# Sparse attention on Trainium2: the value products of a head pair in one burst behind its last probability copy

## The chip, the cores and the metric

The kernel runs on one core of a Trainium2 chip. The metric is the device time of one execution in microseconds. The kernel before takes 2106.75 us, the median of three runs (2106.66 to 2107.36).

## What is computed

The reference is a decoder trunk of two layers on 512 tokens of width 1024, batch 1. Each layer has a hybrid mixer with three branches (sparse attention, HGRN2, gated delta net), a cross attention over 256 memory tokens and a gated MLP with a causal convolution. The change touches only the sparse attention, the branch `nsa_attention`, of which this is the core:

```python
s_cmp = jnp.einsum('bsghd,bngd->bghsn', q, kc).astype(F32) * scale
p_cmp = masked_softmax(s_cmp, cmp_mask)
o_cmp = jnp.einsum('bghsn,bngd->bsghd', p_cmp.astype(vc.dtype), vc)
...
    p = masked_softmax(s, mask)
    return jnp.einsum('bgqhn,bgqnd->bgqhd', p.astype(vg.dtype), vg)
...
p_win = masked_softmax(s_win, wmask[None, :, None, None])
o_win = jnp.einsum('bnghqk,bnkgd->bnqghd', p_win.astype(vw.dtype), vw).reshape(B, S, G, HG, DH)
...
o = g[..., 0:1] * o_cmp + g[..., 1:2] * o_sel + g[..., 2:3] * o_win
```

There are 8 heads of width 64 in 2 groups. Each head's output is a gated sum of three attentions: over 31 compressed blocks, over the selected blocks and over a window. With 512 tokens the selection takes every block and the window every earlier token, so both of these are causal attentions over at most 512 keys.

## The kernel before

**Stages.** Work is tiled into 128 partitions and blocks of 128 tokens. In each layer the mixer runs the gated delta net and HGRN2, then the sparse attention (`nsa_attn`, called from `mixer`), then the gates and branch products that merge the three branches. Dense projections are matmuls of 512 columns (`pd` tiles, helpers `dense` and `mm3`). Each weight block of 128x512 is loaded by SyncE's queue into `wr`, cast by ScalarE to `wh` (line 242) and its remainder is formed by VectorE in `wl` (line 245). Twelve matmuls use one such block. All matmuls go through the helper `mm`, so they stand under line 235. Below, a "dense step" is one matmul into `pd`.

**Order.** The kernel is written as a dataflow. A scheduler with priorities sets the order on each engine when the program is built. Dense matmuls that are due after the attention fill TensorE wherever the attention's own next matmul isn't yet ready by that scheduler's estimate. On each engine the order is then fixed, and an engine waits at the head of its queue.

**The attention.** `nsa_attn` loops over four blocks of queries (i = 0 to 3) and in each over four head pairs (j; one head of each group, g = 0 and 1). That makes 16 rounds in a layer, 32 in all; below, "round" is one (i, j). At the start of a block, compressed scores of all heads are made (`kcT`, eight matmuls), normalized, transposed (line 1065) and copied to `pc`. A round then does this:

- For each g and each of the two attentions br (0 selected, 1 window), scores of width (i+1)*128 (at least 256) are made in a PSUM tile `pa`: two matmuls and a mask product of the bf16 constants `identb` and `negb`. VectorE takes the negated maximum (line 1083) and scales it, ScalarE takes the exponential with its sum into a tile `pr` from the pool `chain`.
- VectorE scales each `pr` by the gate over the sum. TensorE transposes it in i+1 pieces (line 1099) into a PSUM tile `pt`. ScalarE copies that to a further `chain` tile, `pT`.
- The output `po` is a PSUM tile `pa`. Its first two products are those of the compressed values (`vcpad`, one for each g), then come the value products against `tok`: for br 0 and 1, for each key block k, for g 0 and 1. Group 0 writes partitions 0 to 63, group 1 partitions 64 to 127, so each of these matmuls has 64 output rows. ScalarE copies `po` to `y[j]`.

PSUM has three buffers of `pd`, two of `pa` and three of `pt`; `chain` has 36. The products with `vcpad` and `tok` and the transposes are fp32. Each of those products stands as two records in the trace, and each transpose as one.

```python
def mm(out_, lhsT, rhs, start=True, stop=True):
    TE.matmul(out_, lhsT, rhs, start=start, stop=stop, skip_group_check=True)
def pa():
    return pp.tile([P, T], F32, tag="pa", name=f"pa_{uid[0]}", bufs=2)
def pt():
    return pp.tile([P, T], F32, tag="pt", name=f"pt_{uid[0]}", bufs=3)
```

Of the kernel before, what the change touches and what calls it, by code (L numbers as in the profile page):

```python
# [13 lines left out]
AF = mybir.ActivationFunctionType  # L14
# [5 lines left out]
P = 128  # L20
# [178 lines left out]
def tile_trunk(ctx, tc, a, out, dbg=None):  # L199
    nc = tc.nc  # L200
    dbg = dbg or {}
    V, S, G, TE = nc.vector, nc.scalar, nc.gpsimd, nc.tensor
# [7 lines left out]
    def tl(tag, bufs, shape=(P, T), dt=F32):  # L210
        uid[0] += 1
        return sb.tile(list(shape), dt, tag=tag, name=f"{tag}_{uid[0]}", bufs=bufs)

    def chain():
        return tl("chain", NCHAIN)
# [5 lines left out]
    def pa():  # L221
        uid[0] += 1
        return pp.tile([P, T], F32, tag="pa", name=f"pa_{uid[0]}", bufs=2)

    def pt():
        uid[0] += 1
        return pp.tile([P, T], F32, tag="pt", name=f"pt_{uid[0]}", bufs=3)

    def small(n, dt=F32):
        if n <= 16:  # L230
            return tl("tiny", 40, (P, 16), dt)[:, :n]
        return tl("small", 10, (P, 64), dt)[:, :n]

    def mm(out_, lhsT, rhs, start=True, stop=True):
        TE.matmul(out_, lhsT, rhs, start=start, stop=stop, skip_group_check=True)  # L235
# [5 lines left out]
    def act(o, i, f=AF.Copy, **kw):  # L241
        S.activation(o, i, f, **kw)  # L242

    def tt(o, x, y, op, eng=None):
        (eng or V).tensor_tensor(o, x, y, op)  # L245

    def ts(o, x, s1, s2, op0, op1=None, eng=None):
        if op1 is None:
            (eng or V).tensor_scalar(o, x, s1, None, op0)
        else:  # L250
            (eng or V).tensor_scalar(o, x, s1, s2, op0, op1)
# [6 lines left out]
    def mark(name):  # L258
        if "mark" in dbg:
            dbg["mark"](name, nc)  # L260
# [193 lines left out]
    vcpad = [cst.tile([P, 4, 64], F32, name=f"vcpad{i}") for i in range(2)]  # L454
# [571 lines left out]
    def nsa_attn(l, tok, y, st):  # L1026
        KH, KL, QS, kcT, r8 = (st[k] for k in ("KH", "KL", "QS", "kcT", "r8"))
        mark("attn")
        gall = tl("gall", 1, (P, NT, 24))
        act(gall, tok[:, :, TOK_G:TOK_G + 24], AF.Tanh, scale=0.5)  # L1030
        ts(gall, gall, 0.5, 0.5, MUL, ADD)

        for i in range(NT):
            qs_ = slice(i * P, (i + 1) * P)
            sc = pa()
            for j in range(4):
                for g_ in range(2):
                    mm(sc[:, (4 * g_ + j) * 64:(4 * g_ + j + 1) * 64], QS[j, g_][:, qs_],
                       kcT[:, g_].rearrange("p a n -> p (a n)"))
            e = tl("tg", NTG)[:, :256].rearrange("p (h n) -> p h n", h=8)  # L1040
            m3 = cmpm[:, i:i + 1, :].to_broadcast([P, 8, 32])
            pen = tl("cmpn", 1, (P, 32))
            ts(pen, cmpm[:, i, :], -NEG, NEG, MUL, ADD)
            p3 = pen[:, None, :].to_broadcast([P, 8, 32])
            s4 = sc.rearrange("p (h a n) -> p h a n", a=2, n=32)
            tt(e, s4[:, :, 0], p3, ADD)
            tt(e, e, s4[:, :, 1], ADD)
            b8 = lambda t_, n_=32: t_.rearrange("p (h o) -> p h o", o=1).to_broadcast([P, 8, n_])
            tt(e, e, b8(r8[:, i]), MUL)
            mx = small(8)  # L1050
            V.tensor_reduce(mx, e, AX.X, MAX)
            tt(e, e, b8(mx), SUB)
            act(e, e, AF.Exp)
            tt(e, e, m3, MUL)
            dn = small(8)
            V.tensor_reduce(dn, e, AX.X, ADD)
            ts(dn, dn, 1e-30, None, MAX)
            V.reciprocal(dn, dn)
            g3 = gall[:, i, :].rearrange("p (h b) -> p h b", b=3)
            cf = small(8)  # L1060
            tt(cf, dn, g3[:, :, 0], MUL)
            tt(e, e, b8(cf), MUL)
            ps = pt()
            for g_ in range(2):
                TE.transpose(ps[:, g_ * P:(g_ + 1) * P], e[:, g_ * 4:g_ * 4 + 4, :].rearrange("p h n -> p (h n)"), ident)
            pc = tl("tg", NTG)
            act(pc[:, :256], ps[:, :256])

            for j in range(4):
                hd = {}  # L1070
                W = (i + 1) * P
                WM = max(W, 256)
                den = small(4)
                prs = []
                for g_ in range(2):
                    for br in range(2):
                        q_ = QS[j, g_][:, qs_]
                        ps = pa()
                        mm(ps[:, :WM], q_, KH[br, g_][:, :WM], stop=False)
                        mm(ps[:, :WM], q_, KL[br, g_][:, :WM], start=False, stop=False)  # L1080
                        mm(ps[:, i * P:W], identb, negb, start=False, stop=True)
                        nm = small(1)
                        V.tensor_reduce(nm, ps[:, :W], AX.X, MAX, negate=True)  # L1083
                        rc = r8[:, i, 4 * g_ + j:4 * g_ + j + 1]
                        tt(nm, nm, rc, MUL)
                        pr = chain()
                        act(pr[:, :W], ps[:, :W], AF.Exp, bias=nm, scale=rc, accum_out=den[:, 2 * g_ + br:2 * g_ + br + 1])
                        prs.append(pr)
                V.reciprocal(den, den)
                g4 = gall[:, i, :].rearrange("p (g j b) -> p g j b", g=2, b=3)[:, :, j, 1:]  # L1090
                tt(den.rearrange("p (g b) -> p g b", g=2), den.rearrange("p (g b) -> p g b", g=2), g4, MUL)
                for g_ in range(2):
                    for br in range(2):
                        x_ = 2 * g_ + br
                        pr = prs[x_]
                        ts(pr[:, :W], pr[:, :W], den[:, x_:x_ + 1], None, MUL)
                        pst = pt()
                        for k in range(i + 1):
                            TE.transpose(pst[:, k * P:(k + 1) * P], pr[:, k * P:(k + 1) * P], ident)  # L1099
                        pT = chain()  # L1100
                        act(pT[:, :W], pst[:, :W])
                        hd[g_, br] = pT
                po = pa()
                o_ = [po[g_ * 64:(g_ + 1) * 64, :P] for g_ in range(2)]
                for g_ in range(2):
                    mm(o_[g_], vcpad[g_][:, j, :], pc[:, g_ * P:(g_ + 1) * P], start=True, stop=False)
                for br, off in ((0, TOK_VS), (1, TOK_VW)):
                    for k in range(i + 1):
                        for g_ in range(2):
                            mm(o_[g_], tok[:, k, off + g_ * 64:off + g_ * 64 + 64], hd[g_, br][:, k * P:(k + 1) * P],  # L1110
                               start=False, stop=(br == 1 and k == i))
                act(y[j][:, qs_], po[:, :P])
                yield

# [92 lines left out]
    def mixer(l, norm):  # L1207
# [68 lines left out]
        for _ in nsa_attn(l, tok, ya, st):  # L1276
            pass
# [165 lines left out]
```

## Time and profile before

| what | value |
|---|---|
| median of three runs | 2106.75 us |
| the profiled execution's own time | 2107.62 us |
| its span, first to last instruction | 2105.8 us |
| TensorE matmuls busy | 2055.6 us, 98% |
| TensorE weight loads busy | 1611.4 us, 77% |
| VectorE busy | 1436.6 us, 68% |
| ScalarE busy | 952.2 us, 45% |
| GpSimd busy | 132.7 us, 6% |
| mean granted TensorE clock | 0.995 of full speed |

The profiled execution stands 0.87 us over the median. Its own time is 1.8 us more than its span. The attention's rounds lie at about 369 to 556 us in the first layer and 1400 to 1590 us in the second. A matmul's end in the profile is modelled, so a record's length holds time in which the next one already runs. What a matmul costs is read from the step between starts.

### The profile page before, as it was taken

To read this page: it belongs to the slowest core of one execution; us is meant where nothing else is said; L and a number is where in the kernel's file an instruction comes from. 1 tells how busy PE (TensorE), PEld (TensorE's weight loads), DVE (VectorE), ACT (ScalarE), POOL (GpSimd) and SP (SyncE) were. 2 spreads that over 40 slices of the span, in tenths; PEclk is the share of its full clock that TensorE was granted. 3 is DMA by queue.
4 is the path that set the end of the run, shared out by engine and by line. 5 is a ranking of instruction groups with operands and counts; after the bars stand their busy time and mean duration, and the time that the engine had idled before them with its cause. 6 is when DMAs were issued, how large, how long until landed. Compare 5 with 4: busy or idle time off the path is not lost. (4 is left out here: it accounts for less than half of the span.)

```text
span 2105.8 us, 31108 instructions
## 1 busy us (share of the span) xinstructions
PE 2055.6 (98%) x11396; PEld 1611.4 (77%) x11400; DVE 1436.6 (68%) x3052; ACT 952.2 (45%) x1868; POOL 132.7 (6%) x120
## 2 busy tenths in 40 slices
PE   8999999999999999999999998999999999999999
PEld 7877777777786788888888776777778767888887
DVE  6774898666656887377548469975666578755873
ACT  6434434555545544244444244445554454433442
POOL 2000122000010100000000003110000110000000
PEclk9999999999999999999999999999999999999999
DMA  7332222111241233323432312121113412333333
GB/s 238 90 101 71 76 72 61 56 51 46 61 136 47 94 94 95 95 95 96 119 107 78 101 41 91 56 76 51 41 46 91 128 58 90 96 93 98 95 98 108
DMA packets 118826, 180.91 MB, mean 86 GB/s; under 512 B 19920, under 2 KB 40528, under 8 KB 118672
## 3 DMA queue, kind: packets, MB, share of 16 engines
q1 hardware_dynamic: 91008, 158.64, 24.8%
q10 hardware_dynamic: 27584, 19.97, 3.2%
q8 instruction: 90, 1.47, 0.3%
q14 instruction: 64, 0.52, 0.1%
q0 software_dynamic: 80, 0.29, 0.0%
HBM read 170.21 MB, written 8.65 MB: 85 GB/s over the span
## 5 line engine op out<-in xcount | busy, mean ns | idle before, releaser
L235 PE MATMUL pd<-act,wh 128*128 128x512 f32 x3008 | 984.4, 403 | 1.4 <-DVE act L254 1.0
L242 ACT ACTIVATE wh<-wr 128x512 fp32r<-128x512 f32 (+3 forms) x600 | 368.1, 614 | 660.2 <-PE pd L235 578.3
L235 PEld LDWEIGHTS pd<-act,wh 128*128 128x128 f32 x3008 | 559.9, 189 | 133.6 <-issue 15.6
L235 PE MATMUL pd<-act,wl 128*128 128x512 f32 x1504 | 605.8, 403 | 3.0 <-DVE wl L245 3.0
L245 DVE TENSOR_TENSOR wl<-wr,wh 128x512 fp32r<-128x512 f32 (+3 forms) x600 | 409.7, 684 | 209.5 <-ACT wh L242 202.3
L235 PE MATMUL pd<-chain,wh 128*128 128x512 f32 x1344 | 426.1, 397 | 3.4 <-DVE gate L254 3.2
L235 PEld LDWEIGHTS pd<-act,wl 128*128 128x128 f32 x1504 | 284.1, 189 | 72.4 <-issue 7.1
L235 PEld LDWEIGHTS pd<-chain,wh 128*128 128x128 f32 x1344 | 251.9, 189 | 63.0 <-DVE gate L254 3.6
L235 PE MATMUL pd<-chain,wl 128*128 128x512 f32 x672 | 267.3, 398 | 0.9 <-DVE wl L245 0.9
L245 DVE TENSOR_TENSOR gate<-pd,rb 128x512 f32<-128x512 f32 x168 | 116.1, 691 | 103.9 <-PE pd L235 101.7
L235 PE MATMUL pa<-chain,chain 128*64 128x64 f32 (+7 forms) x1248 | 158.0, 294 | 4.6 <-DVE tiny L1340 3.8
L235 PEld LDWEIGHTS pd<-chain,wl 128*128 128x128 f32 x672 | 126.9, 189 | 32.2 <-DVE wl L245 2.9
L254 DVE SCALAR_TENSOR_TENSOR gate<-gate,vec,gate 128x510 f32<-128x510 f32 (+1 forms) x176 | 131.7, 750 | 18.9 <-ACT gate L242 15.9
L235 PEld LDWEIGHTS pa<-chain,chain 128*64 128x64 f32 (+3 forms) x1248 | 109.7, 162 | 43.1 <-issue 16.1
L1083 DVE TENSOR_REDUCE tiny<-pa 128x1 f32<-128x128 f32 (+3 forms) x128 | 61.2, 488 | 81.5 <-PE pa L235 81.2
L242 ACT ACTIVATE chain<-pa,tiny,r 128x128 f32<-128x128 f32 (+3 forms) x128 | 78.8, 616 | 60.9 <-DVE tiny L245 56.4
L245 POOL TENSOR_TENSOR chain<-chain,t 128x512 f32<-128x512 f32 x30 | 40.9, 1362 | 1015.7 <-ACT t L242 1015.7
L242 ACT ACTIVATE chain<-pt 128x512 f32<-128x512 f32 (+3 forms) x156 | 61.0, 444 | 65.0 <-PE pt L1099 37.1
L242 ACT ACTIVATE gate<-gate,vec 128x512 f32<-128x512 f32 x88 | 63.9, 726 | 27.0 <-DVE gate L245 27.0
L245 DVE TENSOR_TENSOR chain<-pd,chain 128x512 f32<-128x512 f32 x64 | 43.7, 688 | 37.0 <-PE pd L235 36.6
L235 PE MATMUL pa<-chain,tok 128*64 128x128 f32 x704 | 62.3, 282 | 0.0
L254 DVE SCALAR_TENSOR_TENSOR t<-t,gate 128x512 f32<-128x512 f32 x88 | 60.6, 688 | 1.9 <-ACT t L242 0.4
(238 smaller groups left out, 2006.4 us busy)
## 6 DMA issues: line engine op xcount, KB each, us to landing
wr<-in_w_fm SPq DMA_DIRECT2D x184, 256.0 KB, 2.7
wr<-in_w_up SPq DMA_DIRECT2D x176, 256.0 KB, 2.6
wr<-in_w_dn SPq DMA_DIRECT2D x64, 256.0 KB, 2.7
wr<-in_w_mix SPq DMA_DIRECT2D x32, 256.0 KB, 2.7
wr<-in_w_dn SPq DMA_DIRECT2D x32, 192.0 KB, 2.4
wr<-in_w_tk SPq DMA_DIRECT2D x16, 272.0 KB, 3.0
wr<-in_w_kv SPq DMA_DIRECT2D x16, 256.0 KB, 3.5
chain<-in_cmp_w SPq DMA_DIRECT2D x16, 256.0 KB, 4.0
```

The lines of the kernel that those rows point to most:

```text
L235: TE.matmul(out_, lhsT, rhs, start=start, stop=stop, skip_group_check=True)
L242: S.activation(o, i, f, **kw)
L245: (eng or V).tensor_tensor(o, x, y, op)
L254: V.scalar_tensor_tensor(o, x, s, y, op0, op1)
L1083: V.tensor_reduce(nm, ps[:, :W], AX.X, MAX, negate=True)
```

## The change

In every round the value products become one block behind the last of the four probability copies, and the compressed products move from its front to its end. Concretely:

- The copy of the transposed probabilities goes back into `pr`, no longer into a new `chain` tile.
- `po` is a `pt` tile, one of the three buffers of the transposes, no longer a `pa` tile, one of the two buffers of the scores.
- The first product of each group (br 0, k 0) gets an added wait on the fourth copy (g 1, br 1), and carries the start flag.
- The `vcpad` products come last.

```diff
-                        pT = chain()
-                        act(pT[:, :W], pst[:, :W])
-                        hd[g_, br] = pT
-                po = pa()
+                        copied = S.activation(pr[:, :W], pst[:, :W], AF.Copy)
+                        hd[g_, br] = pr
+                po = pt()
                 o_ = [po[g_ * 64:(g_ + 1) * 64, :P] for g_ in range(2)]
-                for g_ in range(2):
-                    mm(o_[g_], vcpad[g_][:, j, :], pc[:, g_ * P:(g_ + 1) * P], start=True, stop=False)
                 for br, off in ((0, TOK_VS), (1, TOK_VW)):
                     for k in range(i + 1):
                         for g_ in range(2):
-                            mm(o_[g_], tok[:, k, off + g_ * 64:off + g_ * 64 + 64], hd[g_, br][:, k * P:(k + 1) * P],
-                               start=False, stop=(br == 1 and k == i))
+                            m_ = TE.matmul(o_[g_], tok[:, k, off + g_ * 64:off + g_ * 64 + 64],
+                                           hd[g_, br][:, k * P:(k + 1) * P],
+                                           start=(br == 0 and k == 0), stop=False, skip_group_check=True)
+                            if br == 0 and k == 0:
+                                tc.add_manual_dep(m_.ins, copied.ins.name, mybir.DependencyInfo(
+                                    mybir.DependencyClass.Sync, mybir.DependencyReason.DATA), reason="one burst")
+                for g_ in range(2):
+                    mm(o_[g_], vcpad[g_][:, j, :], pc[:, g_ * P:(g_ + 1) * P], start=False, stop=True)
                 act(y[j][:, qs_], po[:, :P])
```

The scheduler lays the whole attention out anew. Outside the attention, and the dense matmuls around it, the order on TensorE stays. The next rows show three places. They are of the round i = 2, j = 2 of the first layer.

TensorE before, around the compressed products (`vcpad`) of this round, into `pa_4740`:

```order
L235 MATMUL pd_5665<-chain_3168,wl_5662 128x512
L235 MATMUL pa_4740<-tg_4505,vcpad_86 64x128
L235 MATMUL pa_4740<-tg_4505,vcpad_87 64x128
L235 MATMUL pd_5675<-act_160,wh_5678 128x512
L235 MATMUL pd_5675<-act_161,wh_5678 128x512
```

They stand alone between dense matmuls, some 20 rows ahead of the round's other products. TensorE before, at the round's last transposes (line 1099) and its first value products (`tok`):

```order
L1099 MATMUL pt_4727<-cm,chain_4699 128x128 x3
L1099 MATMUL pt_4734<-cm,chain_4708 128x128 x3
L235 MATMUL pa_4740<-chain_4717,tok_533 64x128
L235 MATMUL pd_5675<-act_291,wh_5678 128x512
L235 MATMUL pa_4740<-chain_4731,tok_533 64x128
L235 MATMUL pa_4740<-chain_4717,tok_533 64x128
L235 MATMUL pa_4740<-chain_4731,tok_533 64x128
```

The first value product stands right behind the transposes, alone; a dense matmul parts it from the other eleven. TensorE with the change, at the same place of the same round:

```order
L1099 MATMUL pt_4685<-cm,chain_4659 128x128 x3
L1099 MATMUL pt_4691<-cm,chain_4668 128x128 x3
L235 MATMUL pd_5556<-act_246,wh_5559 128x512
L235 MATMUL pd_5556<-act_247,wh_5559 128x512
L235 MATMUL pd_5556<-act_246,wl_5560 128x512
L1107 MATMUL pt_4696<-chain_4641,tok_533 64x128
L1107 MATMUL pt_4696<-chain_4659,tok_533 64x128
```

Three dense matmuls now stand between the last transpose and the first value product. The end of the same block, with the change:

```order
L1107 MATMUL pt_4696<-chain_4650,tok_533 64x128
L1107 MATMUL pt_4696<-chain_4668,tok_533 64x128
L235 MATMUL pt_4696<-tg_4473,vcpad_86 64x128
L235 MATMUL pt_4696<-tg_4473,vcpad_87 64x128
L235 MATMUL pa_4740<-chain_2600,chain_3745 128x384
L235 MATMUL pa_4740<-chain_2601,chain_3745 128x384
```

The twelve value products and the two compressed ones are one block, and scores of the next round follow. ScalarE with the change, in the same round (`chain<-pt` at line 1100 is a probability copy, `chain,tiny<-pa` the exponential of a score):

```order
L242 ACTIVATE wh_5577<-wr_5575 128x512
L1100 ACTIVATE chain_4641<-pt_4673 128x384
L1100 ACTIVATE chain_4650<-pt_4679 128x384
L1100 ACTIVATE chain_4659<-pt_4685 128x384
L1100 ACTIVATE chain_4668<-pt_4691 128x384
L242 ACTIVATE chain_4729,tiny_4712<-pa_4722,tiny_4726,r_769_3697 128x384
```

The four copies follow each other, as they did before; what moved is that each writes the tile that was transposed.

## Rows read from the trace of the kernel before

**Rows 1.** View by stretch: PE, PEld, DVE, ACT (POOL) busy, clock, DMA share, GB/s.

```profile
369.00:556.00 187.00, 186.76 (x1173) 137.51 (x1173) 117.28 (x337) 103.50 (x269) 0.00 (x0) 1.00 0.15 47
556.00:640.00 84.00, 84.00 (x377) 67.97 (x376) 52.65 (x99) 37.02 (x60) 7.75 (x6) 1.00 0.40 128
...
1400.00:1590.00 190.00, 189.55 (x1184) 139.20 (x1183) 119.63 (x342) 103.34 (x269) 0.00 (x0) 1.00 0.16 48
```

**Rows 2.** Longest of TensorE's waits, 1400 to 1590 us: total, times, longest (us).

```profile
PE pd L235 <- DVE wl L245: 0.2, 1, 0.2
```

**Rows 3.** Timeline, TensorE, at compressed products: start, length, what, count.

```profile
465.38 0.40 PE L235 MATMUL pd<-chain,wl 128*128 128x512 f32 x1
465.61 0.39 PE L235 MATMUL pd<-act,wh 128*128 128x512 f32 x1
465.93 0.44 PE L235 MATMUL pa<-tg,vcpad 128*64 128x128 f32 x4
466.30 0.50 PE L235 MATMUL pd<-act,wh 128*128 128x512 f32 x1
466.64 0.39 PE L235 MATMUL pd<-act,wl 128*128 128x512 f32 x1
```

**Rows 4.** Timeline, TensorE, a round of width 384 with parted value products.

```profile
482.05 1.62 PE L1099 MATMUL pt<-cm,chain 128*128 128x128 f32 x12
483.60 0.43 PE L235 MATMUL pa<-chain,tok 128*64 128x128 f32 x2
483.96 0.49 PE L235 MATMUL pd<-act,wh 128*128 128x512 f32 x1
484.39 1.52 PE L235 MATMUL pa<-chain,tok 128*64 128x128 f32 x22
485.84 0.62 PE L235 MATMUL pa<-chain,chain 128*128 128x384 f32 x2
```

**Rows 5.** Timeline, TensorE, dense steps right behind three transposes.

```profile
470.11 0.49 PE L1099 MATMUL pt<-cm,chain 128*128 128x128 f32 x3
470.36 0.71 PE L235 MATMUL pd<-act,wh 128*128 128x512 f32 x2
470.91 0.40 PE L235 MATMUL pd<-act,wl 128*128 128x512 f32 x1
```

**Rows 6.** Timeline, TensorE, a value block of eight records without a wait.

```profile
426.53 0.66 PE L235 MATMUL pa<-chain,tok 128*64 128x128 f32 x8
427.12 0.44 PE L1099 MATMUL pt<-cm,chain 128*128 128x128 f32 x2
```

**Rows 7.** Timeline, TensorE, the last round of the first layer, width 512.

```profile
548.82 1.94 PE L1099 MATMUL pt<-cm,chain 128*128 128x128 f32 x16
550.69 2.35 PE L235 MATMUL pa<-chain,tok 128*64 128x128 f32 x32
552.97 0.50 PE L235 MATMUL pd<-act,wh 128*128 128x512 f32 x1
```

**Rows 8.** Timeline, TensorE, value block of the first round.

```profile
379.42 0.87 PE L235 MATMUL pa<-chain,tok 128*64 128x128 f32 x8
380.22 0.50 PE L235 MATMUL pd<-act,wl 128*128 128x512 f32 x1
```

**Rows 9.** ScalarE by shape, 369 to 556 us: busy, mean ns, idle before.

```profile
L242 ACT ACTIVATE chain<-pa,tiny,r 128x512 f32<-128x512 f32 x16 | 12.4, 778 | 8.3 <-DVE tiny L245 7.1 <-DVE tiny L1290 1.0
...
L242 ACT ACTIVATE chain<-pt 128x512 f32<-128x512 f32 x16 | 8.2, 601 | 6.1 <-PE pt L1099 6.1
```

**Rows 10.** Timeline, ScalarE, the four copies of the last round.

```profile
549.45 2.06 ACT L242 ACTIVATE chain<-pt 128x512 f32<-128x512 f32 x4 [1.95 <-PE pt L1099]
```

**Rows 11.** Timeline, TensorE, dense steps right behind a mask product.

```profile
462.69 0.23 PE L235 MATMUL pa<-negb,identb 128*128 128x128 bf16 x1
462.73 0.48 PE L235 MATMUL pd<-act,wl 128*128 128x512 f32 x1
463.05 0.62 PE L235 MATMUL pd<-act,wh 128*128 128x512 f32 x2
```

## Prediction

> **What bounds the kernel now.** I read the page first, then the busy time by stretch, then who TensorE waits for, then its timeline. The attention's two stages of 187 and 190 us each have TensorE busy for all but 0.2 to 0.5 us [rows 1]. Its longest wait there totals 0.2 us [rows 2]; the first stage shows only such a wait too. VectorE has 117.28 us of work in 187 us and ScalarE 103.50 us [rows 1]. So these stages last as long as TensorE's queue takes. But a matmul's end is modelled, so "busy" hides what a matmul costs, and the steps between starts tell it. A dense step is 0.23 us (465.38 to 465.61) [rows 3]. Where products with 64 output rows stand between dense ones, the steps are longer: 0.32 us going in, 0.37 us for the four records until the next dense start, 0.34 us for that dense step. Three steps take 1.03 us where two dense ones take 0.46 us, so the visit costs 0.57 us [rows 3].
>
> How much of this is the records themselves? A block of eight records takes 0.59 us from its start to the next instruction [rows 6], a block of four 0.37 us [rows 3], so four more records cost 0.22 us. Hence **a visit to 64 rows costs 0.35 us beyond its records**. The order shows 43 visits in a layer's attention before (16 of compressed products, 27 pieces of value products) and 16 with the change, one a round.
>
> **The change, part by part.**
>
> *Compressed products join the block.* In 32 rounds 0.57 us goes and 0.22 us comes: 32 x 0.35 = 11.1 us saved.
>
> *Parted value products become whole.* 27 - 16 = 11 pieces too many a layer, 22 in all. Before, from the start of the last transpose: 0.20 us to the first piece (a row of 16 transposes takes 1.87 us until the next start, 15 steps of 0.11 and this one [rows 7]), 0.36 us to the dense matmul, 0.43 us to the rest [rows 4]: 0.99 us with one dense matmul in it. With the change three dense matmuls stand there: 0.03 us to the first (0.25 less two steps of 0.11), 0.55 us for the next two [rows 5], 0.32 us going in [rows 3]: 0.90 us. The two dense matmuls more would have cost 0.46 us elsewhere, and the piece's two records cost 0.11 us in the block. Saved: 0.99 + 0.46 - 0.90 - 0.11 = 0.44 us, 22 times: 9.7 us.
>
> *Delays inside blocks.* By the price of rows 6 a block of 32 records should take 0.59 + 24 x 0.055 = 1.91 us; it takes 2.28 us [rows 7], 0.37 us more, in six blocks like it: 2.2 us. The first round's eight records take 0.80 us [rows 8] for 0.59, four times: 0.8 us. Some 20 blocks that begin with the second group's product are 0.09 us over (22 records, 1.45 us [rows 4], for 1.36): 1.8 us. A block that starts when all four copies are there, with both groups in turn, has no cause for these: 4.8 us saved.
>
> *The wait that is added.* The block now stands behind the fourth copy, and in TensorE's queue the next round's scores stand behind the block; VectorE, ScalarE and the round after wait for those. The copies of 512 columns end at 551.51 us (549.45 + 2.06) [rows 10], 1.02 us after the last transpose began (550.69 - 0.20) [rows 7]. The cover, three dense matmuls, is 0.90 us as above. In 8 rounds of that width the order has one to five dense matmuls there, some with scores among them, so I take 0.15 us of waiting in each: 1.2 us. Narrower rounds are covered, since their copies are shorter. In six rounds the order puts another ScalarE instruction between the copies, 0.78 us at most (an exponential of 512 columns [rows 9]), partly covered: 0.2 us each, 1.2 us. Together 2.4 us given back. Bounds: nothing, if the cover always holds; and 32 x 0.5 = 16 us, if ScalarE is behind by 0.5 us at every block.
>
> The Trainium skill, TensorEngine Tiling (Array Packing), section PSUM Bottleneck, says that tiling speeds up TensorE but not the emptying of PSUM, so that the copy may become the bottleneck. The trace bears out a part of it: four copies of 512 columns take 2.06 us [rows 10] and their transposes 1.87 us [rows 7]. By the row the copy trails by a tenth of a microsecond or two, which the dense matmuls cover; by the rule it would pace the stage, the second rival below.
>
> *Scores parted by transposes.* In 13 places the new order puts transposes inside a score's three matmuls, which it never did. What leaving and coming back costs isn't in the trace; the nearest row is a dense step behind a mask product, 0.32 us for 0.23 [rows 11], so 0.09 us each: 1.2 us given back (bounds 0 and 13 x 0.35 = 4.6 us).
>
> *At no cost.* The copy into `pr` waits for the transposes, which it must anyway, so nothing new is queued behind it. `po` takes one of three transpose buffers from the block to its copy; the next transposes come after the next scores, microseconds later. If that failed, a group of transposes would wait for one copy of `po`. It leaves both score buffers free for scores, so the rounds' chain on VectorE and ScalarE shortens and fewer dense matmuls are needed to fill it: 403 between the first compressed score and the last block before, 340 and 341 after. These 125 run behind the attention at the same 0.23 us, where TensorE is busy all the time (84.00 of 84.00 us [rows 1]). SyncE's and GpSimd's queues hold the same work in the same order.
>
> **Sum.** 11.1 + 9.7 + 4.8 - 2.4 - 1.2 = 22.0 us. From the profiled execution's own 2107.6 us that leaves 2085.6 us. The median of the runs stands 0.9 us lower, so the prediction is 2084.7 us.
>
> **Rivals.**
>
> *Short waits eat half.* With less dense work in the stage, transposes and blocks reach the head of TensorE's queue before VectorE's scaling or ScalarE's copy is done. At 0.3 to 0.35 us in each of 32 rounds, 10 to 11 us come back: about 2095 us. For it: the cover at the widest rounds is already short by 0.1 us, and the order was laid out by estimates of the scheduler, not by this chip. Against: with longer queues the same estimates left TensorE 0.2 us of visible waiting [rows 2].
>
> *Slower: ScalarE and VectorE pace the rounds.* If the chain score, maximum, exponential, scaling, transposes, copies, block is what lasts 187 us, then the stage keeps its length, TensorE idles in it, and the 125 dense matmuls that left it come on top: 125 x 0.23 = 28.8 us, 2135.5 us. It decides from the point where a stage shortens by less than the 14.5 us of the 63 matmuls that left it: a round would then still take 10.8 us, against 11.7 now (187 / 16) and 10.1 by my sum. This is what the cited rule would make of it. For it: one exponential and one copy of 512 columns take 0.78 and 0.60 us [rows 9], and a round has four of each. Against: both engines have idle time, 37% and 45% of the stage [rows 1], and the second score buffer shortens the very chain.
>
> *More is saved.* If the copies are always covered and the parted scores cost nothing, 3.6 us more goes, and the visits behind a mask product may cost a little more than those I priced: about 2079 us.
>
> That the change doesn't do what it says is ruled out by the order: each round has one block.
>
> **How the numbers follow.** Forecast as summed 0.70, half eaten 0.16, more saved 0.06, the slower rival 0.05, and a mild form of it that ends near no change 0.03. A measurement of this kernel can tell about 0.2%, 4.2 us. Faster by more: 0.70 + 0.16 + 0.06 = 0.92; within: 0.03; slower: 0.05. The range reaches from the third rival with 2 us to spare, 2077 us, to the first, 2096 us. That leaves out the two slow cases and some of each tail.
>
> **What would show it.** Right: in the timeline each round has one run of 12, 20, 28 or 36 records with 64 output rows, at 0.055 us a record, with a dense matmul or scores on either side. The stages shrink to about 161 us. TensorE's waits for the copies (now line 1100) total under 3 us. The compressed products no longer stand alone. Wrong: TensorE idle by 10 us or more in the attention, behind ScalarE or VectorE (first rival); stages that stay above 172 us (second); or blocks whose records step by more than 0.055 us, by which my price of a visit would be the records' own.

## The result, and the profile after

The changed kernel takes 2088.17 us, the median of four runs (2086.58 to 2089.86), beside 2107.03 us for the kernel before on the same chip. The ratio is 0.9915, its 95% interval 0.9902 to 0.9928: faster by 18.9 us. Forecast were 2084.7 us and 22.0 us of gain; the time lies in the range, 3.5 us above the forecast.

The profiled execution took 2089.86 us, its span is 2088.1 us. The view by stretch of the kernel after shows where the span shrank (columns as in [rows 1]; the first and third lines are the attention's two stages, the second the dense work behind the first):

```profile
369.00:531.00 162.00, 161.62 (x1114) 123.24 (x1114) 109.05 (x327) 97.77 (x262) 0.00 (x0) 1.00 0.16 46
531.00:640.00 109.00, 108.81 (x497) 86.78 (x496) 65.79 (x140) 48.14 (x84) 7.75 (x6) 1.00 0.36 114
1382.00:1545.00 163.00, 162.21 (x1097) 123.90 (x1096) 113.34 (x346) 95.68 (x259) 0.00 (x0) 1.00 0.17 49
```

The stages of 187 and 190 us [rows 1] are 162 and 163 us long, and TensorE is still busy for all but 0.4 and 0.8 us. Its waits in the second stage, in total, times, longest, against [rows 2]:

```profile
PE pa L235 <- ACT chain L242: 0.4, 1, 0.4
PE pa L235 <- DVE cmpn L251: 0.3, 1, 0.3
```

No wait for a copy (line 1100) is among them, nor in the first stage. The timeline of TensorE after (start, length, what, count) shows the first round of the first layer, a round of width 384, and the last round with the dense work behind it:

```profile
379.03 0.39 PE L235 MATMUL pd<-act,wh 128*128 128x512 f32 x1
379.35 0.66 PE L1107 MATMUL pt<-chain,tok 128*64 128x128 f32 x8
379.84 0.39 PE L235 MATMUL pt<-tg,vcpad 128*64 128x128 f32 x4
380.16 0.50 PE L235 MATMUL pd<-act,wh 128*128 128x512 f32 x1
...
458.94 1.53 PE L1107 MATMUL pt<-chain,tok 128*64 128x128 f32 x24
460.31 0.39 PE L235 MATMUL pt<-tg,vcpad 128*64 128x128 f32 x4
460.62 0.62 PE L235 MATMUL pa<-chain,chain 128*128 128x384 f32 x2
461.08 0.23 PE L235 MATMUL pa<-negb,identb 128*128 128x128 bf16 x1
...
522.05 1.06 PE L1099 MATMUL pt<-cm,chain 128*128 128x128 f32 x8
522.88 0.48 PE L235 MATMUL pd<-act,wh 128*128 128x512 f32 x1
523.19 0.39 PE L235 MATMUL pd<-act,wl 128*128 128x512 f32 x1
523.42 0.62 PE L235 MATMUL pd<-act,wh 128*128 128x512 f32 x2
523.88 0.40 PE L235 MATMUL pd<-act,wl 128*128 128x512 f32 x1
524.21 1.97 PE L1107 MATMUL pt<-chain,tok 128*64 128x128 f32 x32
526.01 0.39 PE L235 MATMUL pt<-tg,vcpad 128*64 128x128 f32 x4
526.33 0.73 PE L235 MATMUL pd<-act,wh 128*128 128x512 f32 x2
...
528.06 0.39 PE L235 MATMUL pd<-chain,wl 128*128 128x512 f32 x1
528.48 0.72 PE L235 MATMUL pd<-act,wh 128*128 128x512 f32 x2
529.37 0.50 PE L235 MATMUL pd<-act,wl 128*128 128x512 f32 x1 [0.17 <-DVE wl L245]
```

Each round is one block, products of the compressed values at its end. The last one has 36 records in 2.12 us (524.21 to 526.33); before, 32 records took 2.28 us [rows 7] and the four others stood elsewhere. The price of [rows 6] gives 0.59 + 28 x 0.055 = 2.13 us. In the first round twelve records take 0.81 us, where eight took 0.80 [rows 8]. Five dense matmuls cover the copies of the last round. ScalarE's last two copies of it, in the timeline of the kernel after, end at 523.91 us, 0.30 us before the block starts:

```profile
522.82 1.09 ACT L1100 ACTIVATE chain<-pt 128x512 f32<-128x512 f32 x2
```

Where the 17.8 us between the two profiled executions lie is told by the same instruction's start in both traces. The second column of differences is a repeat of the changed kernel on another chip (run e1 below):

| stretch | before, us | after, us | difference | in the repeat |
|---|---|---|---|---|
| up to the first compressed score | 360.9 | 360.4 | -0.5 | +1.9 |
| attention, first layer, to its last value product | 186.5 | 160.4 | -26.2 | -26.1 |
| dense work behind it, to the next norm | 77.7 | 93.1 | +15.4 | +15.5 |
| up to the second layer's first compressed score | 768.3 | 768.0 | -0.3 | -2.8 |
| attention, second layer | 187.1 | 161.2 | -25.9 | -25.9 |
| dense work behind it | 77.7 | 93.8 | +16.1 | +16.1 |
| to the end | 438.0 | 441.5 | +3.5 | +3.8 |

The four stretches that the change touches give 20.6 us, and the repeat agrees within 0.1 us. The other three hold the same instructions in the same order and vary by up to 4 us from one execution to the next, in part with how many stretches of 3.4 us at half clock (1.2 GHz) fall into them: the last one takes 438.0 us in before and in e2, which have none there, and 439.7 in e3, which has one. So below the stretches of one trace are compared first, and medians where they differ by more.

### The profile page after: what moved, and what is told of

Its sections match the earlier page's. It is cut to its first block, busy times and chain, and to the rows that moved or that the text cites. A ratio compares the mean times of both kernels' runs of the same rounds, so it can differ in the third digit from the quotient of the medians.

```text
span 2088.1 us, 31196 instructions
## 1 busy us (share of the span) xinstructions
PE 2036.5 (98%) x11400; PEld 1606.4 (77%) x11400; DVE 1433.0 (69%) x3052; ACT 948.9 (45%) x1868; POOL 132.7 (6%) x120
## 5 line engine op out<-in xcount | busy, mean ns | idle before, releaser
L235 PE MATMUL pa<-chain,chain 128*64 128x64 f32 (+7 forms) x1248 | 162.4, 297 | 4.8 <-DVE tiny L1343 3.8
L254 DVE SCALAR_TENSOR_TENSOR gate<-gate,vec,gate 128x510 f32<-128x510 f32 (+1 forms) x176 | 131.7, 750 | 18.9 <-ACT gate L242 15.9
L235 PEld LDWEIGHTS pa<-chain,chain 128*64 128x64 f32 (+3 forms) x1248 | 109.2, 162 | 46.0 <-ACT chain L242 17.9
L242 ACT ACTIVATE gate<-gate,vec 128x512 f32<-128x512 f32 x88 | 63.8, 725 | 27.4 <-DVE gate L245 27.4
L1100 ACT ACTIVATE chain<-pt 128x128 f32<-128x128 f32 (+3 forms) x128 | 48.1, 438 | 30.9 <-PE pt L1099 24.0
L245 POOL TENSOR_TENSOR tg<-tg,chain 128x256 f32<-128x256 f32 (+1 forms) x42 | 45.5, 1088 | 190.5 <-ACT tg L242 77.9
```

Source lines behind the costliest of these rows:

```text
L254: V.scalar_tensor_tensor(o, x, s, y, op0, op1)
L1100: copied = S.activation(pr[:, :W], pst[:, :W], AF.Copy)
```

## The experiments

**The theory** is the prediction's: TensorE's queue is the bound, and the gain is the visits to 64 rows that go (43 to 16 a layer, 0.35 us each beyond the records) and the delays inside the blocks. **Rivals:** the added wait itself is the gain; or the score buffer that `po` gives back is. To read each trace the same way, every step between starts on TensorE in the two stages was set against its kind's own (dense 0.231 us, transpose 0.109, value record 0.0547, score 0.231, 0.175 or 0.120 by width, mask product 0.039, compressed score 0.112). What is over falls to a visit (going in, leaving, the dense step behind), to the inside of a visit, or to the rest. What a step has over for what stands ahead of it, such as a mask product, is put to the rest. Sums of both layers, in us:

| kernel | visits | over at visits | inside | rest | sum | median, us |
|---|---|---|---|---|---|---|
| before | 86 | 27.4 | 7.8 | 19.9 | 55.1 | 2107.03 |
| after | 32 | 8.9 | 0.0 | 23.1 | 32.0 | 2088.17 |
| e2, `po` alone | 34 | 9.5 | 2.2 | 24.5 | 36.2 | 2089.75 |
| e3, compressed apart | 64 | 20.2 | 0.1 | 21.7 | 42.0 | 2095.18 |
| e6, wait alone | 64 | 19.8 | 0.1 | 23.2 | 43.1 | 2094.04 |
| e8, no wait | 54 | 16.3 | 6.2 | 25.9 | 48.3 | 2103.83 |
| e9, new tile | 32 | 8.4 | 0.0 | 25.2 | 33.7 | 2085.85 |
| e5, pairs | 16 | 4.2 | 0.0 | 22.1 | 26.3 | 2079.41 |
| e11, pairs, new tile | 16 | 4.5 | 0.0 | 26.0 | 30.4 | 2079.45 |
| e12, pairs, no wait | 16 | 4.6 | 0.0 | 21.5 | 26.1 | 2079.73 |

The first score or transpose step behind a block is longer too, by 0.10 us for a score. It stands under the rest (2.1 us before, 1.8 us after); with it a visit costs 0.31 to 0.35 us on average in every row.

The kernel before took 2106.42 us beside e1 to e4, 2106.05 beside e5 to e8, and 2105.90 beside e9 to e12.

### e1: the changed kernel again

> The changed kernel once more, beside the others. Every theory: between 2086 and 2090 us. Question: the profile has a stretch of 3.4 us at half clock at 1679 us that the kernel before has not there. If it belongs to the program, every execution has it and the time stays at 2089 to 2090 us; if it comes and goes, executions near 2086.6 us stand beside those near 2089.6 us, as in the four runs shown.

2089.72 us (2085.52 to 2090.12), ratio 0.9916 (0.9902 to 0.9929). Both occur: three executions near 2089.8 us and one at 2085.5. The one traced, of 2090.12 us, has the stretch at half clock too, at 1678.5 us; whether it is what the quick one lacks isn't shown. The last section returns to it.

### e2: `po` among the transposes, alone

Of the kernel before:

```diff
-                po = pa()
+                po = pt()
```

> The kernel before with one edit: po is a buffer of the transposes. The compressed products stay in front of the value products, no wait is added, the copies go to new tiles. By the order on TensorE the visits to 64 rows fall from 43 to 17 in a layer, 52 in all. Theory of the visits (0.35 us each beyond its records): 52 x 0.35 = 18.2 us saved, and of the 4.8 us of delays inside blocks none to all: 2084 to 2089 us. Rival, the added wait makes the blocks whole and quick: without it the delays behind the copies stay inside the blocks and only the joined compressed products help, 32 x 0.35 = 11.1 us, about 2096 us. Rival, the score buffer that comes free is the gain: this edit alone is it, 2087 to 2089 us, and then the kernel with po among the scores must lose it.

2089.75 us, ratio 0.992 (0.9906 to 0.9934). One word gives most of the gain, and the rival by which the wait makes it (2096 us) falls. By the order, blocks now begin with the compressed products, in 14 of 17 visits right behind the transposes, and 15 of 16 rounds a layer have one block. But the table says by what it gains: 52 visits fewer are 17.9 us, 0.34 each. The timeline of TensorE in this kernel, last round of the first layer, shows the block behind its transposes:

```profile
524.55 1.97 PE L1099 MATMUL pt<-cm,chain 128*128 128x128 f32 x16
526.46 0.44 PE L235 MATMUL pt<-tg,vcpad 128*64 128x128 f32 x4
526.73 2.08 PE L235 MATMUL pt<-chain,tok 128*64 128x128 f32 x32
528.74 0.72 PE L235 MATMUL pd<-act,wh 128*128 128x512 f32 x2
```

Its 36 records take 2.28 us, 0.16 more than with the change: the copies are awaited inside. That is the 2.2 us under "inside". Over the four stretches the changed kernel is 4.6 us ahead of this one (20.5 against 15.9 us of gain); the medians on that chip, 0.03 us apart, don't show it, since the other three stretches are 7 us shorter in e2's trace.

### e3: the compressed products apart

Of the changed kernel, the core of the edit:

```diff
+                for g_ in range(2):
+                    mm(o_[g_], vcpad[g_][:, j, :], pc[:, g_ * P:(g_ + 1) * P], start=True, stop=False)
                 for br, off in ((0, TOK_VS), (1, TOK_VW)):
...
-                for g_ in range(2):
-                    mm(o_[g_], vcpad[g_][:, j, :], pc[:, g_ * P:(g_ + 1) * P], start=False, stop=True)
```

> The changed kernel with the compressed products at the front again, where they stand alone: 32 visits a layer instead of 16, the same records, the same wait for the fourth copy, po among the transposes. Theory of the visits: 32 x 0.35 = 11.2 us more than the changed kernel, 2099 us. Rival, the wait and the whole block are the gain, and a visit costs no more than its records: 2088 to 2091 us. Rival, the free score buffer is the gain: 2088 to 2091 us as well.

2095.18 us, ratio 0.9947 (0.9935 to 0.9960), 5.5 us over the changed kernel's median on that chip. The median is half of what was expected. The stages' traces, free of what varies outside them, say 10.0 us (42.0 - 32.0), and 11.3 us at the visits: 0.35 us for each of 32, the prediction's price. The four stretches are 9.4 us longer than the changed kernel's, the other three 2.5 us shorter, 1.9 of it at the end, where the changed kernel has a slower dense step (last section). Both rivals (no more than 2091 us) fall. A visit without any wait, in this kernel's timeline on TensorE:

```profile
449.83 1.68 PE L1099 MATMUL pt<-cm,chain 128*128 128x128 f32 x12
451.44 0.44 PE L235 MATMUL pt<-tg,vcpad 128*64 128x128 f32 x4
451.81 0.61 PE L235 MATMUL pa<-chain,chain 128*128 128x384 f32 x2
```

What the price comes from isn't shown. The number format alone it isn't: the transposes are fp32 as the products are, yet in the trace of before going in costs 0.09 us from a transpose and 0.10 from a dense matmul, and leaving 0.15 us towards either. A change of mode fits a rule: the Trainium skill, TensorEngine Tiling (Array Packing), section Key Properties, says that changing the tiling mode drains TensorE. It gives no price; these runs give 0.31 to 0.35 us a visit on average.

### e4: the changed kernel with `po` in a score buffer

```diff
-                po = pt()
+                po = pa()
```

> The changed kernel with po in a score buffer again. The order has 16 visits a layer as in the changed kernel, but 438 dense matmuls in the attention's stage instead of 340. Theory of the visits: the dense matmuls cost the same there as behind the attention, 2086 to 2090 us. Rival, the free score buffer is the gain: most of the 18.9 us comes back, 2100 us or more, with TensorE idle in the attention behind ScalarE or VectorE.

2133.41 us, ratio 1.0129 (1.0113 to 1.0144): the slowest way to have 16 visits a layer, and a miss for the visits alone. The view by stretch of this kernel shows that the loss sits at the end of each stage (first 162 us, then the last 41 us of the first layer):

```profile
369.00:531.00 162.00, 161.39 (x1005) 122.90 (x1003) 105.50 (x301) 87.93 (x228) 0.00 (x0) 1.00 0.19 59
531.00:572.00 41.00, 27.37 (x203) 21.04 (x200) 17.62 (x46) 19.49 (x43) 0.00 (x0) 0.88 0.03 7
```

TensorE's waits from 530 to 573 us, and its timeline there:

```profile
PE pt L1099 <- DVE chain L249: 5.7, 2, 2.9
PE pa L235 <- ACT chain L242: 4.0, 3, 1.3
PE pd L235 <- ACT chain L242: 2.5, 1, 2.5
PE pa L1107 <- ACT chain L1100: 1.4, 2, 0.7
```

```profile
558.49 0.71 PE L235 MATMUL pa<-chain,chain 128*128 128x512 f32 x2
559.04 0.23 PE L235 MATMUL pa<-negb,identb 128*128 128x128 bf16 x1
560.62 0.73 PE L235 MATMUL pa<-chain,chain 128*128 128x512 f32 x2 [1.34 <-ACT chain L242]
561.19 0.23 PE L235 MATMUL pa<-negb,identb 128*128 128x128 bf16 x1
```

With one score buffer taken by `po`, the order has more dense matmuls in a round: 144 over the four rounds of the third block of queries in the first layer, where the changed kernel has 75. At the last rounds they are used up: 438 stand in the stage, and the last three rounds have none, none and six. Rounds without any are called bare below. From mask product to mask product these take 13.3 to 13.6 us. A score waits 1.3 us for the exponential that frees its buffer, the transposes 2.9 us for VectorE's scaling, and the products 0.7 us for the last copy. Is it the buffer, or that the dense work runs out? e6 keeps the buffer taken and the dense work to the end; e7 runs out with the buffer taken, e10 with it free.

### e6: the wait alone, and e7: the compressed products last, alone

e6 is the kernel before with the copy back into `pr` and the added wait of the change, nothing else of it. e7, of the kernel before:

```diff
-                for g_ in range(2):
-                    mm(o_[g_], vcpad[g_][:, j, :], pc[:, g_ * P:(g_ + 1) * P], start=True, stop=False)
...
-                               start=False, stop=(br == 1 and k == i))
+                               start=(br == 0 and k == 0), stop=False)
+                for g_ in range(2):
+                    mm(o_[g_], vcpad[g_][:, j, :], pc[:, g_ * P:(g_ + 1) * P], start=False, stop=True)
```

> The kernel before with the wait alone: the value products stand behind the fourth copy, which goes back into the tile that was transposed; po is a score buffer, the compressed products stay apart in front. The order has 32 visits a layer instead of 43 and 432 dense matmuls in the attention, at least 17 a round to the end. Theory of the run-out (the kernel with po among the scores was slow because its last rounds have no dense matmul left): here they have, so 22 visits fewer at 0.31 us are 6.8 us and the delays inside blocks 4.8 us: 2094 to 2100 us. Rival, the wait with po in a score buffer makes the chain of the rounds the bound whatever stands beside it: 2115 us or more, with TensorE waiting in the attention.

> The kernel before with one edit: the compressed products come last in their block; no wait is added, po is a score buffer. The order has 26 and 28 visits in the layers instead of 43, but the dense matmuls run out: none in the last two rounds of either layer and 8 in the one ahead. Theory of the visits alone: 32 x 0.31 = 9.9 us less than before, 2096 us. Theory of the run-out: the last two rounds of a layer lose 4 us or so each, as in the kernel with po among the scores, and eat the gain: 2107 us or more.

e6: 2094.04 us, ratio 0.9944 (0.9922 to 0.9965). e7: 2127.17 us, ratio 1.0105 (1.0085 to 1.0126). Both have `po` in a score buffer and 432 dense matmuls in the stage. The views by stretch, of e6's whole first stage and of e7's last two rounds there:

```profile
369.00:556.00 187.00, 186.77 (x1203) 138.29 (x1203) 121.71 (x349) 105.34 (x272) 0.00 (x0) 1.00 0.16 52
```

```profile
537.00:569.00 32.00, 21.56 (x144) 16.53 (x143) 14.63 (x40) 14.81 (x32) 0.00 (x0) 0.81 0.05 17
```

In e6, which spreads its dense matmuls to the end, TensorE waits for 0.3 us in both stages together. In e7 it is busy for 21.56 of 32 us, and the granted clock falls to 0.81. So the buffer is not what bounds these kernels; running out of dense work is. e3 and e6 differ by the buffer alone, and neither runs out: ratios 0.9947 and 0.9944, with 324 and 432 dense matmuls in the stage. So what the free buffer does, by the order, is make the rounds take less of the dense work. In bare rounds it is worth little: in e10 below the second and third round of width 512 are bare too, but `po` is among the transposes. From first mask product to first mask product they take 8.9 to 10.2 us without their value products, against e4's 13.3 to 13.6 us, of which 2.8 are such products and the wait for their copies.

### e8: the changed kernel without the wait

The `add_manual_dep` call and its condition are left out.

> The changed kernel without the added wait: po is a transpose buffer, the compressed products come last. The order has 27 visits a layer instead of 16, 324 dense matmuls in the attention. Theory of the visits: 22 x 0.31 = 6.8 us more than the changed kernel, and 2 us of delays inside blocks as in the run with po alone: 2096 to 2099 us. Rival, the wait costs what it saves: 2087 to 2091 us.

2103.83 us, ratio 0.9994 (0.9981 to 1.0007): by the times no gain over the kernel before, and 5 us worse than expected. Its four stretches are 4.2 us shorter than before's, but its dense steps between the two attentions are slower (last section). By the table 7.4 us are visits (22, 0.34 each) and 6.2 us delays inside blocks, where I had put 2; another 2.8 us is the rest, in which dense matmuls wait for VectorE's `wl` (1.6 us in each stage). The timeline of TensorE at a round of width 512 shows a lone first product with a dense matmul and two score products behind it, and then the block:

```profile
517.68 1.11 PE L1099 MATMUL pt<-cm,chain 128*128 128x128 f32 x8
518.73 0.43 PE L1107 MATMUL pt<-chain,tok 128*64 128x128 f32 x2
519.09 0.50 PE L235 MATMUL pd<-act,wh 128*128 128x512 f32 x1
519.43 0.62 PE L235 MATMUL pa<-chain,chain 128*128 128x512 f32 x2
519.98 1.85 PE L1107 MATMUL pt<-chain,tok 128*64 128x128 f32 x29
```

In e2's order the compressed products, which need no copy, stand in front, and the block follows whole. Once they come last, the first value product takes their place behind the transposes, alone, and only the wait joins it to the rest.

### e5: pairs, and e12: pairs without the wait

e5 keeps the probabilities of two head pairs and issues both rounds' products as one block into one `po` tile of 256 columns, behind the fourth copy of the second round. The core of it:

```diff
+                hds[j] = hd
+                if j % 2 != 1:
+                    yield
+                    continue
                 po = pt()
-                o_ = [po[g_ * 64:(g_ + 1) * 64, :P] for g_ in range(2)]
+                for jj in range(j - 1, j + 1):
+                    o_ = [po[g_ * 64:(g_ + 1) * 64, (jj % 2) * P:(jj % 2 + 1) * P] for g_ in range(2)]
```

e12 is e5 without the `add_manual_dep` call.

> The changed kernel with one block for two rounds: the probabilities of two head pairs are kept, and one po tile holds both pairs' products. The order has 8 visits to 64 rows in a layer instead of 16, and 312 dense matmuls in the attention instead of 340, at least 12 in every round, so the dense work does not run out. Theory of the visits at the 0.31 us that the run with the compressed products apart showed: 16 x 0.31 = 5.0 us less than the changed kernel, 2083 to 2085 us. Rival, waits take their place (two rounds of copies before a block, more buffers held): no gain, 2088 to 2092 us.

> One block for two rounds without the added wait: 8 visits a layer as with it, 310 dense matmuls, six of the eight blocks right behind the transposes. Here the wait is taken away with the visits kept. Theory: what is lost are only the delays inside blocks, 1 to 3 us: 2080 to 2083 us, and the wait's worth in the changed kernel lies mostly in the visits that it joins. Rival, the wait itself keeps other matmuls out of TensorE's way: 2085 us or more, as in the kernel without it and with single rounds.

e5: 2079.41 us, ratio 0.9876 (0.9855 to 0.9897). e12: 2079.73 us, ratio 0.9865 (0.9845 to 0.9885). Both beat the changed kernel. With 16 visits fewer 4.7 us go, 0.29 each (0.36 with the score steps behind blocks), and its stages give 5.7 us. The rest of the difference of the medians, against 2088.17 or 2089.72 us, lies outside them; the traces show some 2.7 us of it as the changed kernel's slower dense step. Two rounds of width 512 are one block of 72 records in 4.08 us, in e5's timeline:

```profile
514.30 1.97 PE L1114 MATMUL pt<-chain,tok 128*64 128x128 f32 x32
516.10 0.39 PE L235 MATMUL pt<-tg,vcpad 128*64 128x128 f32 x4
516.32 1.92 PE L1114 MATMUL pt<-chain,tok 128*64 128x128 f32 x32
518.06 0.39 PE L235 MATMUL pt<-tg,vcpad 128*64 128x128 f32 x4
518.38 0.72 PE L235 MATMUL pd<-chain,wh 128*128 128x512 f32 x2
```

With the visits kept the wait is worth nothing (e12): the rival by which it keeps other matmuls out of the way falls. In the changed kernel, then, it is worth the visits and the delays that it removes.

### e9 and e11: the copies in new tiles

Of the changed kernel (e9) and of the pairs (e11):

```diff
-                        copied = S.activation(pr[:, :W], pst[:, :W], AF.Copy)
-                        hd[g_, br] = pr
+                        pT = chain()
+                        copied = S.activation(pT[:, :W], pst[:, :W], AF.Copy)
+                        hd[g_, br] = pT
```

> The changed kernel with the copies in new tiles, as before. 16 visits a layer and the wait stay; by the order 3 scores a layer are parted by other matmuls instead of 9 and 7, and 362 dense matmuls stand in the attention instead of 340. Theory that the parted scores and the transposes beside them are what the attention gave back (some 4.8 us of single steps in the changed kernel's trace): the two stages become 1 to 3 us shorter, 2085 to 2088 us. Rival, where the copy goes and what parts a score cost nothing: the stages stay within 0.5 us.

> One block for two rounds, and the copies in new tiles: 8 visits a layer, 388 dense matmuls in the attention, at least 14 a round, 1 parted score a layer. Theory: as the pairs (2079.4 us), less what the parted scores cost: 2076 to 2079 us. Rival, more dense matmuls in the stage means it is nearer to the run-out, or nothing hangs on parted scores: 2079 to 2083 us.

e9: 2085.85 us, ratio 0.9902 (0.9886 to 0.9917), not to be told from the changed kernel. e11: 2079.45 us, ratio 0.9876 (0.9861 to 0.9891), as the pairs. With 6 parted scores instead of 16, and with 2 in e11, the rest is 2.1 and 3.9 us larger than in the changed kernel and in the pairs, not smaller. So the parted scores are not what the attention gave back; the theory of this run falls. What grew are short delays: steps more than 0.04 us over what is usual behind their neighbour. In sum they are 8.2 us in the changed kernel and 10.4 in e9, 8.0 us in the pairs and 11.6 in e11. Most of them end right behind a release by ScalarE or VectorE, or are the step after such a one. What e9 does save is behind the attention: 82 dense matmuls moved there instead of 125, and 0.3 us lost instead of 2.7.

### e10: one block for four rounds

As e5, with 4 in place of 2.

> The changed kernel with one block for all four rounds of a block of queries: 4 visits a layer. The order puts 286 dense matmuls beside one round of the second block of queries, and from the third on the attention has 32 and then none. Theory of the visits alone: 24 x 0.35 = 8.4 us less than the changed kernel, 2080 us. Theory of the run-out: seven rounds a layer without dense matmuls, each losing 4 us or more as the bare rounds before did: 2130 us or more.

2160.36 us, ratio 1.0260 (1.0245 to 1.0276). The fewest visits (8 in all) make the slowest kernel. The view by stretch of its last 75 us in the first layer:

```profile
505.00:580.00 75.00, 54.12 (x365) 42.69 (x366) 38.77 (x116) 39.71 (x96) 0.00 (x0) 0.82 0.02 4
```

## Why the prediction was right, point by point

| term of the sum | forecast | measured in the traces |
|---|---|---|
| visits: compressed products joined, parted products whole | 11.1 + 9.7 = 20.8 | 21.1 |
| delays inside blocks | 4.8 | 5.7 |
| wait for the fourth copy | -2.4 | -0.4 |
| scores parted by transposes; all other steps | -1.2 | -3.2 |
| 125 dense matmuls moved behind the attention | 0 | -2.7 |
| sum | 22.0 | 20.5 |

- **Visits.** The price held: at the visits 18.6 us went, 19.0 without the 0.4 us of waiting; 2.1 us of the 7.8 us inside belong to the lone pieces (20 x 0.105), which the prediction had priced with them. e3 (0.35 us), e6 against before (0.35) and e2 (0.34) agree. (One reading was short: [rows 7] give 0.22 us, not 0.20, to the first piece, 0.4 us in all.)
- **Delays inside blocks.** Right in kind, sized by three rows where a few more blocks had them.
- **The wait.** The cover held: going in took more than the usual 0.33 us in six rounds only, by 0.4 us together and 0.13 at most, where 2.4 were put down. The dense matmuls that the order puts between the last transpose and the block suffice.
- **The rest** was mis-named. Parted scores are not its cause (e9, e11). In the changed kernel more dense matmuls stand directly behind transposes (48 for 23, each some 0.09 us longer, partly made up by a quicker start), which accounts for 1.4 us. The short delays told of at e9 make up the other 1.8 us but for 0.1: they are 6.5 us before and 8.2 after. No run varied them alone.
- **"At no cost"** failed: the dense matmuls moved behind the attention wait for their weights. The rows of the timeline after show it at 528.06 to 528.48 and 528.48 to 529.37 us, steps of 0.42 and 0.89 us (for two) where 0.23 each is the rule: 0.9 us in the first layer. In the second it is 1.8 us, of which 0.6 is the slower dense step of the last section. The timeline of ScalarE and VectorE there, in the kernel after:

```profile
527.79 1.15 ACT L242 ACTIVATE wh<-wr 128x512 fp32r<-128x512 f32 x2 [0.41 <-PE pd L235]
528.03 0.69 DVE L245 TENSOR_TENSOR gate<-pd,rb 128x512 f32<-128x512 f32 x1
528.63 1.28 DVE L245 TENSOR_TENSOR wl<-wr,wh 128x512 fp32r<-128x512 f32 x2
```

  The cast into `wh` waits for TensorE, and VectorE does a product of the gates before the remainder `wl`. So TensorE busy all the time [rows 1] did not say that more dense work would go there at 0.23 us.
- **The other 1.6 us** between 20.5 and the 18.9 us of the medians are within what the interval of the ratio leaves open (15 to 21 us of gain). Between the two traced executions 2.7 us of loss lie outside the four stretches, which the prediction took as fixed.
- **Luck.** That the sum came within 1.5 us is partly luck: the wait was put 2.0 us too high and the other steps 2.0 us too low. The two large terms, visits and delays inside blocks, don't depend on it: 25.6 us forecast, 26.8 measured.

Of the rivals, short waits that eat half did not come; short waits that eat a tenth did (0.4 us at the blocks and some 1.7 us at scores and transposes). The slower one did not come either, but e4, e7 and e10 are what it looks like: TensorE idle behind ScalarE and VectorE. Its point was mis-stated. What decides is not only how long the chain lasts, but whether the dense matmuls that cover it are used up before the last round. The rule that the prediction cites (the Trainium skill, TensorEngine Tiling (Array Packing), section PSUM Bottleneck) is stated there for a fourfold speed-up of TensorE. Here the copies hold TensorE up by 1.4 us in e4's bare rounds, beside 5.7 us for VectorE's scaling and 4.0 for the exponential; its remedy, both engines emptying PSUM, wasn't tried.

## What to carry to other kernels

Where TensorE's queue is the bound, count the changes of output rows: each visit to 64 rows cost about 0.35 us here, whatever its length, and joining blocks paid until the covering work ran short. When dense work is used as cover, count how much there is and how much each round takes by the order. The stages here with nine dense matmuls or more from each round's last mask product to the next's lost little by waiting. Those with bare rounds lost some 45 us in both layers together (e4 against the changed kernel), though e4's last round still had six. An order is to be read for both before a wait or a buffer is judged.

## What the runs showed of the hardware that was not expected

- **Bare rounds also lose the clock.** In e4, e7 and e10 the granted clock of the bare stretches is 0.88, 0.81 and 0.82: stretches of 3.4 us or more at 1.2 GHz, behind rounds with waits of 1.3 to 3 us. The wait is paid again in slower matmuls: 16 transposes in such a stretch of e4 take 3.32 us (from 565.48 us), 1.97 us at full clock in e2 (from 524.55 us).
- **The same dense work can step slower without any wait.** In the two traces of the changed kernel the dense steps from about 1550 us to the end take 0.2327 us on average; in the traces of before, e2 and e3 they take 0.2314, in the same order of instructions, and no other trace has the slower step there. Over 260 us, TensorE's first column in the views of before, of after and of the repeat:

```profile
1820.00:2080.00 260.00, 260.00 (x1125) 211.28 (x1124) 163.83 (x244) 98.70 (x157) 0.00 (x0) 1.00 0.33 99
```

```profile
1802.00:2062.00 260.00, 260.00 (x1119) 210.63 (x1118) 162.37 (x243) 98.22 (x156) 0.00 (x0) 1.00 0.33 98
```

  1119 matmuls (1119 in the repeat as well) instead of 1125 at a granted clock of 1.00: some 2 us up to the end. ScalarE's and VectorE's instructions keep their lengths. e4 and e8 have the same slower step, 0.2327 us, from the end of their first attention to the second, and 0.2314 again behind that. So it begins and ends in an attention's stage and lasts in between. What sets it is open, and it is most of what the changed kernel lost behind its second attention; a stretch of 3.4 us at half clock at 1678.8 us is the other part, 1.4 us.
- **A visit costs the same ahead of a score.** Behind a block a score starts after 0.20 us as a dense matmul does, and its first product is 0.10 us longer, as the dense one is by 0.11. In the timeline after, the two score products behind a block take 0.46 us to the next start (460.62 to 461.08), where two take 0.35 by their kind's own step. A dense step behind a mask product is longer by 0.09 us as well [rows 11], so this part of a visit may be the price of following another kind of matmul.
